# A hybrid SSD and gMLP layer on one core: the scan's TensorE order is paced by blocks of gate logits

## The chip, the cores and the metric

The kernel runs on one core of one Trainium2 chip. A core has TensorE (PE, with its weight loads PEld), VectorE (DVE), ScalarE (ACT), GpSimd (POOL) and SyncE (SP), on whose queue this kernel issues all its DMAs. Each engine works through its own instructions in the order in which they were written, and waits for others by semaphores. The metric is the device time of one execution in microseconds (us).

## The reference

One layer runs over 1152 positions: 1024 latent tokens (8 chunks of 128) and 128 context tokens (a ninth chunk), width 1024. What matters here:

```
P  = h @ w_in                       # z | x,B,C | dt | u,v | gate logits gA,gB
xbc = silu(depthwise_conv(x,B,C))
per chunk, direction, head:  decay = exp(segment sums of dt*a)
  y_diag = (C B^T * decay * dt) x ;  y_off = (C * exp(acum)) h_start
  h_next = exp(a_last) * h + (B * decay_to_end * dt)^T x
y_a = rms_norm((y_fwd + y_bwd + d_skip*x) * silu(z))
u,v = gelu(..) ; v = layer_norm(v) ; y_b = u * (w_spatial v + b)
m  = sigmoid(gA) * (y_a @ w_proj_a) + sigmoid(gB) * (y_b @ w_proj_b)
x  = LN(alpha x + gate1 * (m @ w_out)) ; then a squared-relu MLP and a second LN
```

Latent tokens start from given states, one for each direction; context tokens start from zero, and their final states are outputs.

## The kernel before

Activations lie in SBUF as feature tiles of 128 features by 1152 positions, cut into three blocks of 384 positions. All large products use fp32r operands that are split into a high and a low part, so that one product is three matmuls (`mm3`, L89 to L92). A block of one weight tile is 8 x 3 = 24 matmuls of 128x384 (`fm_block`, L203). Weight tiles of 128x1024 come by DMA (`more_raw`); ScalarE makes the high part and GpSimd or VectorE the low part (`split`, L81 to L87).

The order of the stages: modulation and the first two x/B/C weight tiles, whose products run feature tile by feature tile beside the loading (L373 to L390); the dt chain (`dt_chain`, L415), whose cumulative sums go to DRAM as FB and whose transposes on TensorE (L447) fill QT; ten more x/B/C tiles with convolution and transposes (L465 on); the scan (L528 to L629); the gate logits, 16 weight tiles with 48 blocks of 24 matmuls (L632 to L641), which depend on nothing in the scan; then z (24 blocks), v with its layer norm, u with the spatial product (L743 to L762), the projections and the MLP.

The scan has a backward pass: for chunks 7 to 1 `advance` (L548) multiplies the state `hst` by `eal` on GpSimd (L554), forms the chunk's contribution on TensorE (L551) and adds it on VectorE (L555), while each state is written to DRAM as HB. Then the final states of the context chunk are formed (L562 to L571). The forward pass (L574) goes through chunks 0 to 7 and last the context chunk, each in four steps of four heads, 36 steps in all. One step, on the tiles Fb, Bb (cumulative sums, loaded by DMA and broadcast), Ef and cbD:

```
ACT   Ef = exp(Fb)                    (L599, latent chunks)
DVE   Fb -= QT  (L601);  4x Fb = min(Bb - QT, Fb)  (L604)
POOL  4x cbD = cbU * dt  (L606);  DVE 4x cbD += cbL * dt  (L607)
ACT   Fb = exp(Fb) (L609), Bb = exp(Bb) (L612);  DVE Fb *= cbD (L610)
POOL/DVE Ef *= C (L614, every other step on each), POOL Bb *= C (L615)
PE    y = Fb x + Ef h + Bb h_bwd  (L624);  ACT copies y over x (L626)
```

A scheduler in the framework lays the program out into the engines' queues: it mixes gate-logit matmuls between the scan's small products where it holds the scan's operands to be late. `order(ins, first)` (L140) ties one instruction behind another in that layout without a semaphore. Tiles of a pool rotate over `bufs` buffers; a writer waits until the last reader of its buffer is done.

## Time and profile before

| | |
|---|---|
| runs | 2047.31, 2158.1 and 7596.76 us (median 2158.1) |
| the profiled execution's own time | 2048.03 us |
| its span | 2046.2 us, mean granted TensorE clock 0.982 |
| PE busy | 1932.7 us (94%) |
| DVE busy | 1272.4 us (62%) |
| POOL busy | 689.1 us (34%) |
| ACT busy | 607.1 us (30%) |
| chain that ended last | PE 64%, DVE 22%, DMA 5%, issue 4%, POOL 2%, ACT 2% |

Busy is the time in which an engine had an instruction in work; an engine's successive instructions overlap a little, so that the mean time of one is longer than the step from one start to the next. The chain is followed back from the last instruction to what released it. The shares are means over stages that differ, so the stage that a change touches has to be looked at by itself: the scan lies between about 215 and 541 us of the span, the gate logits between 215 and 557, z from there to about 660, and v and u behind it.

### The profile page before, as it was taken

The page shows a single profiled execution, that of the slowest core. Times are in us where ns is not written, and L with a number is a line of the kernel's source. Part 1 is how long each engine was busy: PE and PEld are TensorE (multiplying, and loading weights), DVE is VectorE, ACT ScalarE, POOL GpSimd, SP SyncE. Part 2 cuts the span into 40 slices and gives each one's busy share as a digit, 9 for nine tenths or more (in the row PEclk, how much of TensorE's full clock was granted, in tenths as well). Part 3 has the DMA queues.
Part 4 walks back from the last instruction along what each step waited for, and adds up shares of the span by engine and source line. Part 5 has one row for each costly group of instructions (what it writes and reads, how often), then busy time and mean ns, then how long its engine had stood idle before and what let it go on. Part 6 is the DMA issues. An engine that isn't in the chain of part 4 may idle for free.

```text
span 2046.2 us, 27658 instructions
## 1 busy us (share of the span) xinstructions
PE 1932.7 (94%) x10669; PEld 1759.5 (86%) x10669; DVE 1272.4 (62%) x2171; ACT 607.1 (30%) x1010; POOL 689.1 (34%) x560
## 2 busy tenths in 40 slices
PE   7999998787899999999999999999999999999886
PEld 4899897676899779999998889899999999988775
DVE  4556837999599534344465875754444444458998
ACT  3333313333322332143232453121221111123423
POOL 0323414767224450046120134511122111135563
PEclk9999999899999999999999999999999999999998
DMA  8145435444485431159544543611111111125432
GB/s 319 34 144 167 169 128 176 117 148 126 131 267 164 135 104 62 42 164 342 160 139 159 199 172 130 223 58 42 42 42 42 48 46 42 42 82 182 138 123 83
DMA packets 110213, 262.47 MB, mean 128 GB/s; under 512 B 11584, under 2 KB 50176, under 8 KB 108928
## 3 DMA queue, kind: packets, MB, share of 16 engines
q1 hardware_dynamic: 110080, 260.70, 38.9%
q8 instruction: 84, 1.38, 0.3%
q14 instruction: 49, 0.40, 0.1%
HBM read 213.30 MB, written 47.35 MB: 127 GB/s over the span
## 4 chain that ended last, share of the span: by engine, by line
PE 64%; DVE 22%; DMA 5%; issue 4%; POOL 2%; ACT 2%; SPq 1%; POOLq 0%; DVEq 0%; ACTq 0%
PE mm_ps L91 20%; PE mm_ps L90 20%; PE mm_ps L92 20%; DVE Fb L604 2%; DVE cbD L607 2%; DMA w_raw<-in_w_ff_dram 1%; DVE crow L282 1%; DVE Fb L601 1%; DMA xg<-NX 1%; DVE w_lo L87 1%; DMA Fb<-FB 1%; DVE Fb L610 1%; DVE xg L934 1%; DVE acc L1021 1%; DVE ln_t L248 1%
## 5 line engine op out<-in xcount | busy, mean ns | idle before, releaser
L87 POOL TENSOR_TENSOR w_lo<-w_raw,w_hi 128x1024 fp32r<-128x1024 f32 x88 | 214.5, 2443 | 517.3 <-ACT w_hi L82 513.7
L82 ACT ACTIVATE w_hi<-w_raw 128x1024 fp32r<-128x1024 f32 (+2 forms) x199 | 205.3, 1039 | 541.5 <-PE mm_ps L92 299.7
L90 PE MATMUL mm_ps<-hTh,w_hi 128*128 128x384 f32 x1056 | 359.4, 344 | 5.7 <-ACT gt L638 3.9
L92 PE MATMUL mm_ps<-hTh,w_lo 128*128 128x384 f32 x1056 | 363.1, 344 | 1.1 <-POOL w_lo L87 1.1
L91 PE MATMUL mm_ps<-hTl,w_hi 128*128 128x384 f32 x1056 | 361.6, 342 | 0.0
L90 PE MATMUL mm_ps<-h,w_hi 128*128 128x384 f32 x768 | 258.9, 338 | 10.5 <-DVE acc L1021 8.9
L92 PE MATMUL mm_ps<-h,w_lo 128*128 128x384 f32 x768 | 258.9, 337 | 5.2 <-POOL w_lo L85 5.2
L91 PE MATMUL mm_ps<-h,w_hi 128*128 128x384 f32 x768 | 258.5, 337 | 0.0
L1021 DVE TENSOR_TENSOR acc<-acc,mm_ps 128x512 f32<-128x512 f32 x240 | 161.1, 684 | 122.9 <-PE mm_ps L92 122.8
L90 PEld LDWEIGHTS mm_ps<-hTh,w_hi 128*128 128x128 f32 x1056 | 200.5, 190 | 15.7 <-issue 6.8
L91 PEld LDWEIGHTS mm_ps<-hTl,w_hi 128*128 128x128 f32 x1056 | 200.7, 190 | 8.4 <-issue 5.9
L92 PEld LDWEIGHTS mm_ps<-hTh,w_lo 128*128 128x128 f32 x1056 | 200.6, 190 | 8.0 <-issue 6.5
L90 PE MATMUL mm_ps<-w_hi,hid 128*128 128x512 f32 x518 | 200.6, 390 | 4.3 <-DVE acc L1021 3.1
L91 PE MATMUL mm_ps<-w_lo,hid 128*128 128x512 f32 x518 | 202.2, 390 | 2.2 <-POOL w_lo L85 2.1
L92 PE MATMUL mm_ps<-w_hi,hid 128*128 128x512 f32 x518 | 201.4, 389 | 0.0
L983 DVE TENSOR_TENSOR rl<-rl 128x384 f32<-128x384 f32 x96 | 112.2, 1170 | 129.3 <-ACT rl L982 129.2
L90 PEld LDWEIGHTS mm_ps<-h,w_hi 128*128 128x128 f32 x768 | 145.6, 190 | 13.3 <-DVE acc L1021 10.1
L92 PEld LDWEIGHTS mm_ps<-h,w_lo 128*128 128x128 f32 x768 | 145.6, 190 | 5.5 <-POOL w_lo L85 5.5
L91 PEld LDWEIGHTS mm_ps<-h,w_hi 128*128 128x128 f32 x768 | 145.6, 190 | 0.7
L87 DVE TENSOR_TENSOR w_lo<-w_raw,w_hi 128x1024 fp32r<-128x1024 f32 (+2 forms) x78 | 94.6, 1216 | 71.9 <-ACT w_hi L82 71.8
L90 PEld LDWEIGHTS mm_ps<-w_hi,hid 128*128 128x128 f32 x518 | 97.4, 188 | 26.4 <-DVE acc L1021 4.4
L91 PEld LDWEIGHTS mm_ps<-w_lo,hid 128*128 128x128 f32 x518 | 97.4, 188 | 24.0 <-POOL w_lo L85 4.1
(260 smaller groups left out, 3550.8 us busy)
## 6 DMA issues: line engine op xcount, KB each, us to landing
w_raw<-in_w_ff_dram SPq DMA_DIRECT2D x93, 512.0 KB, 3.7
w_raw<-in_w_v_dram SPq DMA_DIRECT2D x24, 512.0 KB, 3.6
w_raw<-in_w_out_dram SPq DMA_DIRECT2D x24, 512.0 KB, 3.7
Fb<-FB SPq DMA_DIRECT2D x36, 256.0 KB, 4.0
Bb<-FB SPq DMA_DIRECT2D x36, 256.0 KB, 4.8
GLOG<-gt SPq DMA_DIRECT2D x48, 192.0 KB, 1.9
gin<-GLOG SPq DMA_DIRECT2D x48, 192.0 KB, 3.1
ada_b<-in_w_ada_dram SPq DMA_DIRECT2D x16, 512.0 KB, 7.5
```

The lines of the kernel that those rows point to most:

```text
L82: A.activation(hi, raw, AF.Copy)
L87: eng.tensor_tensor(lo, raw, hi, op=SUB)
L90: T.matmul(ps, s[0], m[0], start=first, stop=False)
L91: T.matmul(ps, s[0], m[1], start=False, stop=False)
L92: T.matmul(ps, s[1], m[0], start=False, stop=last)
L248: V.scalar_tensor_tensor(t, y, x, y, op0=MUL, op1=MUL)
L282: V.scalar_tensor_tensor(wt[:, i, :] if v else junk, wt[:, i, :], 1.0, crow[:, v, :], op0=MUL, op1=MUL, accum_out=outs[:, k, i, v:v + 1])
L601: V.tensor_tensor(Fb, Fb, QT[:, c, 2, h0:h0 + 4].unsqueeze(2).broadcast_to([P, 4, P]), op=SUB)
L604: V.scalar_tensor_tensor(Fb[:, i, :], Bb[:, i, :], QT[:, c, 3, h:h + 1], Fb[:, i, :], op0=SUB, op1=MIN)
L607: V.scalar_tensor_tensor(cbD[:, i, :], cbL[:, g, :], QT[:, c, 0, h:h + 1], cbD[:, i, :], op0=MUL, op1=ADD)
L983: V.tensor_tensor(rl, rl, rl, op=MUL)
L1021: V.tensor_tensor(a, a, ps, op=ADD)
```

## The change

In the scan: (1) the forward pass takes the context chunk first; (2) the state `hst` has two buffers, and `advance` writes the product with `eal` to the new one, on VectorE (it was in place on GpSimd); (3) the four cbD products of a step, the dt weights, are ScalarE copies with a scale (they were GpSimd's); (4) Ef has two buffers for three, cbL and cbU have one for two; (5) the first y product of each step and the first state product of each backward chunk are tied behind a numbered block of gate logits, so that the 36 steps spread over all 48 blocks. Outside it: (6) the spatial product of u is tied behind the last matmul of its own block; (7) the dt transposes are tied behind the fourth x/B/C tile; (8) the third x/B/C weight tile is loaded and split during the start, into a block buffer.

```diff
--- before.py
+++ after.py
@@ -89,7 +89,7 @@
     def mm3(ps, s, m, first, last):
         T.matmul(ps, s[0], m[0], start=first, stop=False)
         T.matmul(ps, s[0], m[1], start=False, stop=False)
-        T.matmul(ps, s[1], m[0], start=False, stop=last)
+        return T.matmul(ps, s[1], m[0], start=False, stop=last)
 
 
     wsrc = []
@@ -115,7 +115,7 @@
     for i in range(len(FIN)):
         fin += [("f1fin", i, (2,))] + [("w2fin", j, None) for j in range(sum(FIN_W2[:i]), sum(FIN_W2[:i + 1]))]
     plan += fin[:2] + [("f2", NCH - NE, (2,))] + fin[2:]
-    homes, HOME = {}, [0, 0, 0, 1, None, None]
+    homes, HOME = {2: 0}, [0, 0, 0, 1, None, None]
     for op, n, bs in plan:
         if op == "f1fin":
             wsrc.append(("ff1", I["w_ff1"][FIN[n]]))
@@ -203,9 +203,11 @@
     def fm_block(pm, w, act, b, evict):
         ps = pm.tile([P, TB], F32, name="mm_ps", tag="mm")
         for k in range(KT):
-            mm3(ps, (w[0][:, k, :], w[1][:, k, :]), (act[b][0][:, k, :], act[b][1][:, k, :]),
-                k == 0, k == KT - 1)
+            done = mm3(ps, (w[0][:, k, :], w[1][:, k, :]), (act[b][0][:, k, :], act[b][1][:, k, :]),
+                       k == 0, k == KT - 1)
+        state["mm"] = done
         evict(b, ps)
+        return done
 
     def fm_tile(pm, w, act, evict, blocks=range(NB)):
         for b in blocks:
@@ -337,7 +339,7 @@
 
 
     lo_eng["eng"] = lambda i: V
-    BEHIND = {KT - 1: (2, 3)}
+    BEHIND = {3: (2,), KT - 1: (3,)}
     fetch_ada(0)
     dma(out=ident, in_=I["ident"])
     dma(out=posr, in_=I["posr"])
@@ -372,6 +374,8 @@
 
     for k in range(KT):
         ht = fetched[k]
+        if k == 5:
+            first.append(take_fm("xbc", 0, 0))
         if k == 2:
             ada_half(1, aux([P, 512], "ada_ps", "tp", 2))
         sc, sh = mod_cols(k, 1)
@@ -411,6 +415,8 @@
     dtv, e1, e2 = (qt[0:R, i * TB:(i + 1) * TB] for i in range(3))
     e3, sf, sb = (qs[0:R, i * TB:(i + 1) * TB] for i in range(3))
     A.activation(dtv, dtp[0:R, :], AF.Identity, bias=dtb[0:R, :])
+
+    late_pe = []
 
     def dt_chain():
         qm = t1_tile("qm")
@@ -444,7 +450,9 @@
         for src, r0, nr, q in ((dtv, 0, 2, 0), (sf, 0, 1, 2), (sb, 1, 1, 3)):
             tp = aux([P, 3, R], "q_ps", "tp", 2)
             for cc in range(3):
-                T.transpose(tp[:, cc, :], src[:, cc * P:(cc + 1) * P], ident[0:R, 0:R])
+                ins = T.transpose(tp[:, cc, :], src[:, cc * P:(cc + 1) * P], ident[0:R, 0:R])
+                if cc == 0:
+                    late_pe.append(ins)
             for cc in range(3):
                 V.tensor_copy(QT.rearrange("p (b c) r h -> p b c r h", c=3)[:, :, cc, q:q + nr, :],
                               tp[:, cc, :].rearrange("p (b r h) -> p b r h", r=2, h=H)[:, :, r0:r0 + nr, :])
@@ -463,7 +471,7 @@
     CT = bcs.tile([P, 2, W], F32, name="CT")
     Bk = bcs.tile([P, NC, 2 * P], F32, name="Bk")
     for n, ft in enumerate((8, 9, 10, 11, 0, 1, 2, 3, 4, 5, 6, 7)):
-        w = take_fm("xbc") if n > 1 else None
+        w = take_fm("xbc") if n > 2 else first[n]
         if ft == 0:
             X = [blk.tile([P, 3, D], F32, name=f"X{b}", tag="blk", bufs=NBLK) for b in range(NB)]
         cv = cvp.tile([P, CW + 2], F32, name="cv", tag="cv", bufs=3)
@@ -485,6 +493,9 @@
                 dt_chain()
         else:
             fm_tile(pmA, w, hT, ev_x)
+            if n == 3:
+                for ins in late_pe:
+                    order(ins, state["mm"])
         t1 = t1_tile("t1")
         w0, w1, w2 = (conv_wc[i][:, ft:ft + 1] for i in range(3))
         G.tensor_scalar(t1, cv[:, 1:1 + CW], w1, conv_bc[:, ft:ft + 1], op0=MUL, op1=ADD)
@@ -535,7 +546,7 @@
         return X[c // 3][:, c % 3, :]
 
     def load_state(src):
-        hs = sp.tile([P, D], F32, name="hst", tag="hst")
+        hs = sp.tile([P, D], F32, name="hst", tag="hst", bufs=2)
         dma(out=hs, in_=src)
         return hs
 
@@ -545,20 +556,28 @@
                         wfb[:, d, c, g * 8:g * 8 + 8].unsqueeze(2).broadcast_to([P, 8, 64]), op=MUL)
         return xw
 
+
+    paced = []
+
     def advance(hs, c, d, xws):
+        new = sp.tile([P, D], F32, name="hst", tag="hst", bufs=2)
         for g in range(2):
             st = aux([P, 512], "st_ps", "st", 1)
-            T.matmul(st, Bk[:, c, g * P:(g + 1) * P], xws[g].rearrange("p h e -> p (h e)"), start=True, stop=True)
-            hg = hs[:, g * 512:(g + 1) * 512]
-            hv = hg.rearrange("p (h e) -> p h e", e=64)
-            G.tensor_tensor(hv, hv, eal[:, d, c, g * 8:g * 8 + 8].unsqueeze(2).broadcast_to([P, 8, 64]), op=MUL)
+            ins = T.matmul(st, Bk[:, c, g * P:(g + 1) * P], xws[g].rearrange("p h e -> p (h e)"), start=True, stop=True)
+            if d == 1 and g == 0:
+                paced.append((ins, NL - 1 - c))
+            hg = new[:, g * 512:(g + 1) * 512]
+            V.tensor_tensor(hg.rearrange("p (h e) -> p h e", e=64),
+                            hs[:, g * 512:(g + 1) * 512].rearrange("p (h e) -> p h e", e=64),
+                            eal[:, d, c, g * 8:g * 8 + 8].unsqueeze(2).broadcast_to([P, 8, 64]), op=MUL)
             V.tensor_tensor(hg, hg, st, op=ADD)
+        return new
 
     hb = load_state(I["h0_b"])
     for c in range(NL - 1, -1, -1):
         dma(out=HB[c], in_=hb)
         if c > 0:
-            advance(hb, c, 1, [xweight(c, 1, g) for g in range(2)])
+            hb = advance(hb, c, 1, [xweight(c, 1, g) for g in range(2)])
     for d in range(2):
         for g in range(2):
             xw = xweight(NL, d, g)
@@ -571,7 +590,8 @@
             dma(out=ov[:, 4 * g:4 * g + 4, :], in_=fs)
 
     hf = load_state(I["h0_f"])
-    for c in range(NC):
+    LEAD = 8
+    for at, c in enumerate([NL] + list(range(NL))):
         lat = c < NL
         if lat:
             hbc = [sp.tile([P, 512], F32, name="hbc", tag="hbc", bufs=2) for _ in range(2)]
@@ -581,8 +601,8 @@
         cbp = aux([P, 2, P], "cb_ps", "tp", 2)
         for g in range(2):
             T.matmul(cbp[:, g, :], BT[:, g, c * P:(c + 1) * P], CT[:, g, c * P:(c + 1) * P], start=True, stop=True)
-        cbL = sp.tile([P, 2, P], F32, name="cbL", tag="cbL", bufs=2)
-        cbU = sp.tile([P, 2, P], F32, name="cbU", tag="cbU", bufs=2)
+        cbL = sp.tile([P, 2, P], F32, name="cbL", tag="cbL", bufs=1)
+        cbU = sp.tile([P, 2, P], F32, name="cbU", tag="cbU", bufs=1)
         V.tensor_tensor(cbL, cbp, mlu[:, 0:1, :].broadcast_to([P, 2, P]), op=MUL)
         V.tensor_tensor(cbU, cbp, mlu[:, 1:2, :].broadcast_to([P, 2, P]), op=MUL)
         for g in range(2):
@@ -595,7 +615,7 @@
                     dma(out=t.rearrange("p h i -> p (h i)"),
                         in_=FB[c, d, h0:h0 + 4, :].rearrange("h i -> (h i)").partition_broadcast(P))
                 if lat:
-                    Ef = sp.tile([P, 4, P], F32, name="Ef", tag="Ef", bufs=3)
+                    Ef = sp.tile([P, 4, P], F32, name="Ef", tag="Ef", bufs=2)
                     A.activation(Ef, Fb, AF.Exp)
                 cbD = sp.tile([P, 4, P], F32, name="cbD", tag="cbD", bufs=2)
                 V.tensor_tensor(Fb, Fb, QT[:, c, 2, h0:h0 + 4].unsqueeze(2).broadcast_to([P, 4, P]), op=SUB)
@@ -603,7 +623,7 @@
                     h = h0 + i
                     V.scalar_tensor_tensor(Fb[:, i, :], Bb[:, i, :], QT[:, c, 3, h:h + 1], Fb[:, i, :],
                                            op0=SUB, op1=MIN)
-                    G.tensor_scalar(cbD[:, i, :], cbU[:, g, :], QT[:, c, 1, h:h + 1], 0.0, op0=MUL, op1=ADD)
+                    A.activation(cbD[:, i, :], cbU[:, g, :], AF.Copy, scale=QT[:, c, 1, h:h + 1])
                     V.scalar_tensor_tensor(cbD[:, i, :], cbL[:, g, :], QT[:, c, 0, h:h + 1], cbD[:, i, :],
                                            op0=MUL, op1=ADD)
                 A.activation(Fb, Fb, AF.Exp)
@@ -621,14 +641,19 @@
                     for n, (lhs, l0, rhs) in enumerate(terms):
                         for i in range(2):
                             j = 2 * qq + i
-                            T.matmul(yp[64 * i:64 * i + 64, q, :], lhs[:, l0 + 64 * j:l0 + 64 * j + 64], rhs[:, j, :],
-                                     start=n == 0, stop=n == len(terms) - 1)
+                            ins = T.matmul(yp[64 * i:64 * i + 64, q, :], lhs[:, l0 + 64 * j:l0 + 64 * j + 64], rhs[:, j, :],
+                                           start=n == 0, stop=n == len(terms) - 1)
+                            if n == i == qq == 0:
+                                e = 4 * at + 2 * g + hh
+                                paced.append((ins, LEAD * (e + 1) // 4 if at == 0 else
+                                              LEAD + (e - 3) * (6 * KT - LEAD) // 32))
                 A.activation(xch(c)[:, (g * 4 + hh * 2) * P:(g * 4 + hh * 2 + 2) * P],
                              yp[:, 2 * hh:2 * hh + 2, :].rearrange("p a b -> p (a b)"), AF.Copy)
         if c < NL - 1:
-            advance(hf, c, 0, xws)
-
-
+            hf = advance(hf, c, 0, xws)
+
+
+    blocks_done = []
     for kind, g0 in (("gb", 8), ("ga", 0)):
         for ft in range(KT):
             w = take_fm(kind)
@@ -638,7 +663,10 @@
                 A.activation(gt, ps, AF.Copy)
                 dma(out=GLOG[g0 + ft][:, b * TB:(b + 1) * TB], in_=gt)
 
-            fm_tile(pmA, w, hT, ev_g)
+            for b in range(NB):
+                blocks_done.append(fm_block(pmA, w, hT, b, ev_g))
+    for ins, n in paced:
+        order(ins, blocks_done[max(0, n - 1)])
     psA.close()
     stA.close()
 
@@ -746,7 +774,9 @@
         def ev_u(b, ps):
             sps = pxB.tile([P, 3, P], F32, name="s_ps", tag="aux")
             for cc in range(3):
-                T.matmul(sps[:, cc, :], Vh[b][:, cc, g * P:(g + 1) * P], WsT[:, g, :], start=True, stop=True)
+                ins = T.matmul(sps[:, cc, :], Vh[b][:, cc, g * P:(g + 1) * P], WsT[:, g, :], start=True, stop=True)
+                if cc == 0:
+                    order(ins, state["mm"])
             ug = tB.tile([P, TB], F32, name="ug", tag="ta", bufs=2)
             A.activation(ug, ps, AF.Gelu)
             sl = tB.tile([P, 3, P], F32, name="sl", tag="tb", bufs=2)
```

What this does to the order, at three places. First TensorE's queue at the end of the scan, where `mm_ps` are gate-logit or z matmuls and `y_ps` the scan's outputs. Before:

```order
L92 MATMUL mm_ps_4837<-hTh2_215,w_lo_4686 128x384
L90 MATMUL mm_ps_4837<-hTh2_215,w_hi_4685 128x384
L624 MATMUL y_ps_3464<-Fb_3490,X2_855 64x128 x4
L91 MATMUL mm_ps_4837<-hTl2_216,w_hi_4685 128x384
L92 MATMUL mm_ps_4837<-hTh2_215,w_lo_4686 128x384
L90 MATMUL mm_ps_4837<-hTh2_215,w_hi_4685 128x384
```

and now:

```order
L91 MATMUL mm_ps_4940<-hTl2_216,w_hi_4788 128x384
L92 MATMUL mm_ps_4940<-hTh2_215,w_lo_4789 128x384
L644 MATMUL y_ps_3451<-Fb_3490,X2_854 64x128 x2
L644 MATMUL y_ps_3451<-Ef_3494,hst_3354 64x128 x2
L644 MATMUL y_ps_3451<-Bb_3491,hbc_3364 64x128 x2
L644 MATMUL y_ps_3451<-Fb_3490,X2_854 64x128 x2
L644 MATMUL y_ps_3451<-Ef_3494,hst_3354 64x128 x2
L644 MATMUL y_ps_3451<-Bb_3491,hbc_3364 64x128 x2
L90 MATMUL mm_ps_5012<-hTh0_211,w_hi_4878 128x384
L91 MATMUL mm_ps_5012<-hTl0_212,w_hi_4878 128x384
```

Before, the last y product had 83 gate-logit matmuls behind it; now the gate logits end before it, and the next row is the first z matmul.

Second ScalarE's queue at the start, from the last high part of the activations (`hTh`): `qt` belongs to the dt chain, `crow` to the modulation, and the `cv` rows empty the accumulators `mm_ps` and `mm2_ps` of the first two weight tiles. Before:

```order
L82 ACTIVATE hTh2_215<-xt_359 128x384
L401 ACT_TABLE_LOAD
L401 ACTIVATE anc_518<-pcol_76 128x1
L413 ACTIVATE qt_523<-dt_ps_223,pcol_76 96x384
L476 ACTIVATE cv_529<-mm_ps_217 128x384
L476 ACTIVATE cv_529<-mm_ps_218 128x384
L476 ACTIVATE cv_620<-mm2_ps_220 128x384
L476 ACTIVATE cv_620<-mm2_ps_221 128x384
```

and now:

```order
L82 ACTIVATE hTh2_215<-xt_359 128x384
L405 ACT_TABLE_LOAD
L405 ACTIVATE anc_523<-pcol_76 128x1
L417 ACTIVATE qt_528<-dt_ps_223,pcol_76 96x384
L430 ACTIVATE qt_528<-qt_528 96x384
L528 ACT_TABLE_LOAD
L528 ACTIVATE crow_960<-crow_960 128x1024
L484 ACTIVATE cv_534<-mm_ps_217 128x384
L484 ACTIVATE cv_625<-mm2_ps_220 128x384
L484 ACTIVATE cv_534<-mm_ps_218 128x384
L484 ACTIVATE cv_625<-mm2_ps_221 128x384
```

The dt chain's exponential, a table load and the `crow` activation moved ahead of the four rows that empty accumulators.

Third TensorE's queue around the first spatial product, `s_ps`; 128x512 matmuls are v, 128x384 are u. Before:

```order
L90 MATMUL mm_ps_6227<-w_hi_6253,hTh1_213 128x512
L90 MATMUL mm_ps_6228<-w_hi_6253,hTh1_213 128x512
L749 MATMUL s_ps_6816<-WsT_6765,V0_5956 128x128 x3
L91 MATMUL mm_ps_6226<-w_lo_6254,hTh1_213 128x512
L92 MATMUL mm_ps_6226<-w_hi_6253,hTl1_214 128x512
L90 MATMUL mm_ps_6226<-w_hi_6253,hTh1_213 128x512
```

and now:

```order
L91 MATMUL mm_ps_6804<-hTl0_212,w_hi_6683 128x384
L92 MATMUL mm_ps_6804<-hTh0_211,w_lo_6684 128x384
L777 MATMUL s_ps_6829<-WsT_6778,V0_5969 128x128 x3
L92 MATMUL mm_ps_6840<-hTh1_213,w_lo_6684 128x384
L90 MATMUL mm_ps_6840<-hTh1_213,w_hi_6683 128x384
```

It stood 39 matmuls behind the end of the first third of v, inside v; now it stands behind the first block of u, 16 blocks' worth of matmuls later.

## Rows read from the trace of the kernel before

**Rows 1.** Busy time of each engine in two stretches (us, instructions), TensorE's granted clock, DMA.

```profile
328.00:541.00 213.00, 174.44 (x1335) 149.12 (x1337) 200.64 (x373) 74.75 (x153) 143.77 (x178) 0.94 0.47 137
541.00:557.00 16.00, 15.05 (x91) 14.56 (x87) 1.23 (x2) 3.90 (x7) 0.00 (x0) 1.00 0.20 70
```

**Rows 2.** The chain of waits (start, us); then line L638, the gate logits' evictions.

```profile
313.82 1.40 PE y_ps L624 x20
...
L638 ACT ACTIVATE gt<-mm_ps x48: 466/477/495, 221.9 to 556.9; 128x384 f32<-128x384 f32 x48
```

**Rows 3.** VectorE's groups from 328 to 541: count, busy us, mean ns, idle before.

```profile
L607 DVE SCALAR_TENSOR_TENSOR cbD<-cbL,QT,cbD 128x128 f32<-128x128 f32 x124 | 62.2, 542 | 2.8 <-POOL cbD L606 2.8
L604 DVE SCALAR_TENSOR_TENSOR Fb<-Bb,QT,Fb 128x128 f32<-128x128 f32 x124 | 56.5, 511 | 0.9 <-DMA Bb<-FB 0.6
L601 DVE TENSOR_TENSOR Fb<-Fb,QT 128x512 f32<-128x512 f32 x31 | 27.3, 879 | 3.6 <-ACT Ef L599 2.5 <-DMA Fb<-FB 0.9
L610 DVE TENSOR_TENSOR Fb<-Fb,cbD 128x512 f32<-128x512 f32 x32 | 24.5, 768 | 0.8 <-ACT Fb L609 0.7
```

**Rows 4.** GpSimd's groups in the same stretch.

```profile
L606 POOL TENSOR_SCALAR cbD<-cbU,QT 128x128 f32<-128x128 f32 x123 | 66.6, 556 | 18.0 <-DVE Fb L610 18.0
L615 POOL TENSOR_TENSOR Bb<-Bb,CT 128x512 f32<-128x512 f32 x28 | 44.9, 1605 | 34.7 <-ACT Bb L612 31.4 <-DVE Fb L604 2.5 <-DVE Ef L614 0.6
L614 POOL TENSOR_TENSOR Ef<-Ef,CT 128x512 f32<-128x512 f32 x13 | 18.9, 1450 | 5.0 <-ACT Ef L599 5.0
L554 POOL TENSOR_TENSOR hst<-hst,eal 128x512 f32<-128x512 f32 x14 | 15.4, 1099 | 0.0
```

**Rows 5.** VectorE's instructions in order of time: start, us.

```profile
415.70 3.99 DVE L607 SCALAR_TENSOR_TENSOR cbD<-cbL,QT,cbD 128x128 f32<-128x128 f32 x4
...
420.21 0.68 DVE L614 TENSOR_TENSOR Ef<-Ef,CT 128x512 f32<-128x512 f32 x1
420.82 1.21 DVE L87 TENSOR_TENSOR w_lo<-w_raw,w_hi 128x1024 fp32r<-128x1024 f32 x1
421.95 1.13 DVE L604 SCALAR_TENSOR_TENSOR Fb<-Bb,QT,Fb 128x128 f32<-128x128 f32 x4
423.00 0.68 DVE L544 TENSOR_TENSOR xw<-X,wfb 128x512 f32<-128x512 f32 x1
```

**Rows 6.** GpSimd's instructions at the first of these.

```profile
415.61 1.32 POOL L614 TENSOR_TENSOR Ef<-Ef,CT 128x512 f32<-128x512 f32 x1
417.11 1.38 POOL L615 TENSOR_TENSOR Bb<-Bb,CT 128x512 f32<-128x512 f32 x1 [0.18 <-DVE cbD L607]
418.45 1.09 POOL L554 TENSOR_TENSOR hst<-hst,eal 128x512 f32<-128x512 f32 x1
```

**Rows 7.** ScalarE: line L378 (ns, least, median, most); then the y evictions from 328 to 541.

```profile
L378 ACT ACTIVATE xt<-xt,mod x8: 478/480/495, 17.3 to 44.9; 128x128 f32<-128x128 f32 x8
...
L626 ACT ACTIVATE X<-y_ps 128x256 f32<-128x256 f32 x35 | 12.9, 370 | 6.9 <-PE y_ps L624 3.5 <-DVE xw L544 3.4
```

**Rows 8.** TensorE's waits from 560 to 830; then its instructions around the first such wait.

```profile
PE s_ps L749 <- DVE V L719: 6.4, 4, 2.5
...
699.13 0.39 PE L91 MATMUL mm_ps<-w_lo,hTh 128*128 128x512 f32 x1
...
708.75 0.80 PE L749 MATMUL s_ps<-WsT,V 128*128 128x128 f32 x2 [2.45 <-DVE V L719]
...
711.05 0.63 PE L92 MATMUL mm_ps<-w_hi,hTl 128*128 128x512 f32 x1
```

**Rows 9.** Start: TensorE's first matmul of the third weight tile, and two of ScalarE's rows.

```profile
66.74 0.45 PE L90 MATMUL mm_ps<-hTh,w_hi 128*128 128x384 f32 x1 [1.85 <-ACT w_hi L82]
...
68.93 1.28 ACT L517 ACT_TABLE_LOAD   x1
70.23 1.06 ACT L517 ACTIVATE crow<-crow 128x1024 f32<-128x1024 f32 x1
```

**Rows 10.** TensorE's waits from 0 to 310.

```profile
PE q_ps L447 <- DVE qs L437: 1.8, 1, 1.8
```

## The prediction

> **What bounds the kernel now.** The page's busy table says TensorE (94%), but it is a mean over stages. I looked for the stretches in which TensorE is not full, with the busy times by window, and then asked the groups of each engine and the waits why. Three places matter.
>
> The first is the forward pass of the scan. The chain reaches its first y product at 313.82 [rows 2]. From 328 to 541 VectorE is busy 200.64 of 213 us, TensorE 174.44 at a mean granted clock of 0.94, ScalarE 74.75, GpSimd 143.77 [rows 1]: VectorE sets the pace. After it, from 541 to 557, TensorE runs alone (15.05 of 16, VectorE 1.23, GpSimd 0): the gate-logit matmuls that were left when the scan ended. The last gate eviction is at 556.9 [rows 2], so z begins at 557. Gate logits could fill TensorE's holes inside the scan, and 16 us of them are spent behind it.
>
> The second is inside VectorE's 200 us. Its mask and dt-weight operations on 128x128 take 542 and 511 ns in the mean [rows 3]. At a moment without GpSimd, four of them take 1.13, and a 128x512 product takes 0.68 with a step of 0.61 to the next [rows 5]. So one step is about 0.263, one latency 0.34, and the rest of the 511 to 542 is stretch. Taking off 0.34 or 0.68 for each: 25 (L607), 21 (L604), 6 (L601) and 3 (L610), together 55 us of 213. Where three GpSimd tensor operations run (1.32 + 1.38 + 1.09), a group of four took 3.99 instead of 1.13 [rows 5, 6].
>
> The third lies outside the scan: TensorE waits 6.4 us for the normalized v in front of spatial products [rows 8], 1.8 at a dt transpose [rows 10], and 1.85 for the third weight tile [rows 9].
>
> **The change part by part. Sum against the profiled execution's 2048.03 us**, which stands 0.7 above the lowest of the runs, 2047.31; their median, 2158.1, is 5% higher because of the spread between them, and I forecast an execution like the profiled one.
>
> *The scan.* Before, 33 of the 36 steps were left at 314 and the last ended near 541: 6.9 us each. Now context comes first, and the four context steps and one latent step go through VectorE during the backward pass, where TensorE has a gate block for each state product and VectorE has room: 31 are left. TensorE has 654 gate matmuls left at that point. The forward pass starts at about 315: 21 more gate matmuls precede it, at 0.17 (15.05 over 91, 16 over 91 [rows 1]) 3.6 us, less about 2 for state products that no longer wait for GpSimd.
>
> VectorE's clean work from there: 31 steps of eight 128x128 at 0.263 and two 128x512 at 0.6 make 102, less 2 for operations already done; 16 Ef products 10; 14 weightings of x, 14 state additions and 12 state multiplications at 0.6, 24; eight low parts of weights at 1.13, 9; seven pairs of masked cb, 5. Sum 148. The state multiplications are the part newly put on VectorE (7 us, and as much in the backward pass, where it is hidden).
>
> On top comes stretch. GpSimd loses the dt weights (66.6) and the state products (15.4) and keeps Bb and its half of Ef, 44.9 + 18.9 [rows 4], for 31 instead of 28 latent steps 70 us. What stretches VectorE isn't settled by the rows. If every GpSimd microsecond counts alike, 55 over 145.8 is 0.38, and 26 us stay. If only GpSimd's tensor-by-tensor operations count, the group of four gives 2.9 over 3.8, 0.75, and about 50 stay. I take the middle, 37, since both kinds were there in nearly every slow group. With 10 idle (12.4 in 213 before), VectorE needs 148 + 37 + 10 = 195, bounds 184 and 207. The scan ends at 510, its last y takes 1.4 [rows 2], and no gate logits are left behind it: z begins at 512 instead of 557. **Minus 45**, from -56 to -33.
>
> Is TensorE able to follow? 654 x 0.17 = 111, 32 y groups at 1.4, 45, states and cb 8: 165 of the 195. Yes, with 30 spare.
>
> ScalarE gets 144 copies. An eviction of 128x256 without pointers takes 370; 128x128 with two pointers takes 478 to 495 [rows 7]. One pointer on 128 columns lies between, 0.26 (370 less the 107 that the gate eviction's 128 columns more cost, 477 [rows 2]) and 0.48; at 0.36 that is 1.4 us per step on an engine that is busy 75 of 213. Not the bound, but its queue is in order: behind a copy that waits for cbU or for a cbD buffer stand the two exponentials of that step, the next exp(Fb), and the gate evictions. The copies' wait is the same that GpSimd had; who waits for it now is new (a rival below).
>
> By the Trainium skill, "ScalarE: Activation LUTs", section "What ACT_TABLE_LOAD costs", a copy of 128 columns with one pointer would take some 0.39, about 0.29 back to back, an estimate of 42 us for the 144 copies; the two-pointer figure it gives agrees with the 478 to 495 here. The same page's "Rules for kernel authors" would have multiplications on VectorE and not on ScalarE, which speaks against this part; here VectorE is the engine without room.
>
> Ef with two buffers for three, cbL and cbU with one for two: at no cost as long as ScalarE's exp(Fb) is a step ahead; if that cover goes, see the rivals.
>
> *Spatial products.* Two waits, together 6.4 us in four entries at two places, the longest 2.45 at 708.75; behind it 128x512 matmuls take 0.63 instead of 0.39 [rows 8] for about 13 matmuls, 3 us. Tied behind the first block of u, 277 matmuls later, V is long ready. 6.4 + 2 x 3 = 12; I allow 8 to 13, as the second wait is shorter. **Minus 12.** Nothing is late next: the product of the gate in u needs it only with its own block's eviction.
>
> *dt transposes*: the 1.8 goes [rows 10]. **Minus 2.** QT comes later, but is needed only in the scan.
>
> *Third weight tile early.* The 1.85 wait for its high part goes [rows 9]. But ScalarE's four rows that empty the accumulators now stand behind the dt exponential, a table load (1.28) and crow (1.06) [rows 9], and TensorE, with three accumulators, waits for one of these instead: 1.28 + 1.06 + about 0.5 less 1.85, **plus 1**, -3 to +3. The reordered loads on SyncE's queue and the extra low part on VectorE lie beside TensorE's products.
>
> Sum: -45 - 12 - 2 + 1 = -58, **1990 us**; own range 1976 to 2006.
>
> **The rivals.**
> *TensorE becomes the bound (0.13).* All stretch goes with the dt weights, if those alone made it: VectorE needs 148 + 10, and TensorE's 165 decides. z begins at 315 + 165 + 2 = 482, and the sum is -75 - 13 = 1960 to 1965. For: L607 sits right behind L606, and GpSimd was busy with L606 longest. Against: the slow group stood beside L614, L615 and L554, not L606 [rows 5, 6]. The Trainium skill, "SBUF — State Buffer", section "SBUF: two separate sides", says that VectorE with two SBUF inputs and a reading GpSimd block each other wholly, one for the whole length of the other; by this all 82 us taken off GpSimd would come back, up to TensorE's bound. The trace shows less: 55 lost beside 145.8.
>
> *The step keeps its 6.9 us (0.17).* The scan is then bound by the round over ScalarE: Fb's exponential, four copies, two more exponentials and a y copy, in one queue, with fewer Ef buffers. 31 x 6.9 = 214: z at 530, -27 - 13 = 2008. For: 2.5 of L601's 3.6 idle us already wait for ScalarE's Ef [rows 3]. Against: ScalarE is busy 35%.
>
> *Slower (0.04).* The tied y products put a serial chain in TensorE's order: y frees Ef, the exponential two steps on may start, then ScalarE's copies, exp of Fb and Bb, GpSimd's Bb product at 1.6 [rows 4], the next y. Behind the waiting y stand 21 gate matmuls that can't pass it, 3.6 us; so they add to the chain instead of filling it. If the chain is 1.4 for y, 3.6 for the matmuls, 1.4 for the copies, two exponentials at about 0.7 (a 128x512 by the 0.107 per 128 columns from the 0.37 of 128x256 is 0.58) and 1.6 for Bb, it is 9.4 us a step: the scan takes 291, z begins at 606, and the time is 2048 + 49 - 13 = 2084. It decides from a step of (557 + 13 - 315) / 31 = 8.2 us on. Against: the y products are tied to block counts, and the operands of two steps lie ahead.
>
> *The ties do little (0.04)*: the layout was as good before, only the waits outside go; 2035.
>
> **How the numbers follow.** Forecast 0.62 (1976 to 2006), TensorE bound 0.13 (1960 to 1965), step kept 0.17 (2000 to 2020), slower 0.04, little 0.04. The range 1967 to 2022 holds the forecast and the kept step, and leaves out most of the TensorE case and the last two, about 0.2. Two per cent, about what a measurement of this kernel can tell from no change, is 41 us: faster means under 2007. That is the forecast, the TensorE case and a little under half of the kept step, less the forecast's upper edge: 0.79. Slower needs 2089, the far end of its case: 0.03. The rest, 0.18, is within 2%.
>
> **What would show it.** Right: z's first matmul near 512; no stretch with VectorE idle and TensorE on gate logits behind the last y; L604 and L607 near 0.4 in the mean, GpSimd about 70 us in the forward pass; TensorE's clock there nearer to 1; no wait at s_ps and q_ps. Wrong: L604 and L607 still above 0.5 with GpSimd halved (the tensor products make the stretch); y waiting long for Bb or Ef with ScalarE or GpSimd as the releaser (the round); z near 482 (TensorE). The third tile is right if TensorE's longest wait between 60 and 75 names a ScalarE row that empties an accumulator.

## The result, and the profile after

The changed kernel takes 1995.72 us (median of four executions, 1993.56 to 1998.1), 0.9747 of the kernel before, with an interval of 0.9723 to 0.977: 52 us less on 2048. Two executions of before were disturbed and raise its plain median; the ratio leaves them out, as do all ratios below. The forecast was 1990, 58 us less. The total is near by luck: two terms were wrong in opposite directions, and what I named as the cause of the larger one is only a part of it.

The profiled execution has a span of 1996.3 us, 49.9 less than before. First the busy times from the beginning of the gate logits to z (columns as in [rows 1]; the order is TensorE, its weight loads, VectorE, ScalarE, GpSimd, then TensorE's granted clock; the second window ends a microsecond into z):

```profile
215.00:311.30 96.30, 95.44 (x546) 87.63 (x546) 59.19 (x117) 32.52 (x70) 7.55 (x2) 1.00 0.51 173
311.30:517.70 206.40, 185.83 (x1454) 160.36 (x1449) 190.18 (x381) 116.36 (x278) 74.66 (x46) 0.98 0.50 142
```

Then the line of the gate logits' evictions, as in [rows 2]:

```profile
L663 ACT ACTIVATE gt<-mm_ps x48: 466/473/494, 213.1 to 516.2; 128x384 f32<-128x384 f32 x48
```

And VectorE's groups inside the forward pass, 320 to 511, with GpSimd's behind them (count, busy us, mean ns, idle before; compare [rows 3, 4]):

```profile
L624 DVE SCALAR_TENSOR_TENSOR Fb<-Bb,QT,Fb 128x128 f32<-128x128 f32 x119 | 54.3, 510 | 1.1 <-DMA Bb<-FB 0.9
L627 DVE SCALAR_TENSOR_TENSOR cbD<-cbL,QT,cbD 128x128 f32<-128x128 f32 x112 | 42.9, 429 | 3.3 <-ACT cbD L626 3.3
L621 DVE TENSOR_TENSOR Fb<-Fb,QT 128x512 f32<-128x512 f32 x29 | 22.5, 775 | 2.9 <-ACT Ef L619 2.8
L573 DVE TENSOR_TENSOR hst<-hst,st_ps 128x512 f32<-128x512 f32 x14 | 9.5, 676 | 0.0
L570 DVE TENSOR_TENSOR hst<-hst,eal 128x512 f32<-128x512 f32 x12 | 8.9, 770 | 0.0
```

```profile
L635 POOL TENSOR_TENSOR Bb<-Bb,CT 128x512 f32<-128x512 f32 x29 | 48.1, 1659 | 73.4 <-ACT Bb L632 52.3 <-DVE Fb L624 9.9 <-DVE hst L573 6.5
L634 POOL TENSOR_TENSOR Ef<-Ef,CT 128x512 f32<-128x512 f32 x14 | 22.9, 1633 | 47.5 <-ACT Ef L619 47.5
```

What the reader sees: the gate logits begin at 213.1 instead of 221.9, 8.8 us earlier; the forward pass begins at 311.3 instead of 313.8, so 6.3 of the 8.8 are used up before it; z's first matmul starts at 516.8 instead of 557.4. From the first gate eviction to that matmul it was 335.5 us and is 303.7: 31.8 less. From there to the end, 9.3 less: 8.8 + 31.8 + 9.3 = 49.9. VectorE still sets the pace (190 of 206), and the mask operations (L624) are as slow with half of GpSimd's work gone as they were before, 510 ns against 511.

### The profile page after: what moved, and what is told of

Same layout as the page of the kernel before. It is cut to its first block, busy times and chain, and to the rows that moved or that the text cites. A ratio compares the mean times of both kernels' runs of the same rounds, so it can differ in the third digit from the quotient of the medians.

```text
span 1996.3 us, 27629 instructions
## 1 busy us (share of the span) xinstructions
PE 1917.7 (96%) x10669; PEld 1749.4 (88%) x10669; DVE 1263.2 (63%) x2200; ACT 651.7 (33%) x1154; POOL 590.0 (30%) x387
## 4 chain that ended last, share of the span: by engine, by line
PE 67%; DVE 18%; DMA 7%; issue 4%; ACT 2%; POOL 2%; SPq 1%; POOLq 0%; ACTq 0%; DVEq 0%
PE mm_ps L90 21%; PE mm_ps L91 21%; PE mm_ps L92 21%; DMA w_raw<-in_w_ff_dram 2%; DVE Fb L624 2%; ACT w_hi L82 1%; DVE rl L1013 1%; DVE cbD L627 1%; DMA xg<-NX 1%; PE y_ps L644 1%; DVE w_lo L87 1%; DVE crow L284 1%; DMA ada_w<-in_w_ada_dram 1%; DVE xg L964 1%; DVE w_lo L85 1%
## 5 line engine op out<-in xcount | busy, mean ns | idle before, releaser
L90 PE MATMUL mm_ps<-hTh,w_hi 128*128 128x384 f32 x1032 | 355.3, 348 | 0.9 <-ACT gt L663 0.9
L92 PE MATMUL mm_ps<-hTh,w_lo 128*128 128x384 f32 x1032 | 350.6, 340 | 0.7 <-DVE w_lo L87 0.7
L91 PE MATMUL mm_ps<-hTl,w_hi 128*128 128x384 f32 x1032 | 350.3, 339 | 0.0
L90 PEld LDWEIGHTS mm_ps<-hTh,w_hi 128*128 128x128 f32 x1032 | 195.4, 190 | 11.1 <-issue 7.9
L91 PEld LDWEIGHTS mm_ps<-hTl,w_hi 128*128 128x128 f32 x1032 | 194.7, 189 | 9.5 <-issue 7.0
L92 PEld LDWEIGHTS mm_ps<-hTh,w_lo 128*128 128x128 f32 x1032 | 194.5, 188 | 5.3 <-issue 4.3
```

The lines of the kernel that those rows point to most:

```text
L90: T.matmul(ps, s[0], m[0], start=first, stop=False)
L91: T.matmul(ps, s[0], m[1], start=False, stop=False)
L92: return T.matmul(ps, s[1], m[0], start=False, stop=last)
```

## The experiments

Seventeen kernels ran. The effect of each is given in us as the difference of two ratios to before, times 2048; the interval of one ratio is 6 to 11 us wide from end to end, so a difference of less than some 5 to 7 us can't be told from none.

| kernel | ratio to before | interval | against the changed kernel |
|---|---|---|---|
| the change | 0.9747 | 0.9723 to 0.977 | |
| dt weights back on GpSimd (cbd_pool) | 0.983 | 0.9808 to 0.9852 | +17 |
| one state buffer, in place (hst_inplace) | 0.9808 | 0.979 to 0.9826 | +12 |
| spatial products as before (spat_off) | 0.9795 | 0.9768 to 0.9822 | +10 |
| third weight tile as before (third_back) | 0.979 | 0.9773 to 0.9808 | +9 |
| third tile and dt transposes as before (outer_off) | 0.9784 | 0.977 to 0.9799 | +8 |
| context last, ties kept (ctx_last) | 0.9774 | 0.9752 to 0.9796 | +6 |
| context last, no ties (ctx_pace_off) | 0.9766 | 0.9752 to 0.9781 | +4 |
| state product on GpSimd (hst_pool) | 0.9758 | 0.9732 to 0.9784 | +2 |
| dt transposes as before (dt_off) | 0.9754 | 0.9739 to 0.9768 | +1 |
| no ties (pace_off) | 0.9751 | 0.9733 to 0.977 | +1 |
| all products on VectorE (all_dve) | 0.9679 | 0.9657 to 0.97 | -14 |
| and a subtraction on ScalarE (dve_sub_act) | 0.9629 | 0.9608 to 0.9649 | -24 |
| the same without ties (best_nopace) | 0.9633 | 0.9613 to 0.9654 | -23 |

| before, plus | ratio | interval | against before |
|---|---|---|---|
| dt weights on ScalarE (b_cbd) | 0.9984 | 0.9968 to 1.0 | -3 |
| second state buffer (b_hst) | 0.9958 | 0.9943 to 0.9972 | -9 |
| both (b_cbd_hst) | 0.9938 | 0.9914 to 0.9962 | -13 |
| both, state product on VectorE (b_scan) | 0.9872 | 0.9845 to 0.9898 | -26 |

**What stretches VectorE.** First the dt weights taken back:

```
-                    A.activation(cbD[:, i, :], cbU[:, g, :], AF.Copy, scale=QT[:, c, 1, h:h + 1])
+                    G.tensor_scalar(cbD[:, i, :], cbU[:, g, :], QT[:, c, 1, h:h + 1], 0.0, op0=MUL, op1=ADD)
```

> The changed kernel with the dt weights cbD back on GpSimd, all else as changed. Theory (VectorE paces the forward pass, and a GpSimd product stretches it only while a scalar_tensor_tensor wants to start): the 124 dt weights give back about 20 us of stretch to VectorE, less 3 us of waits for ScalarE: 2008 to 2016 us. Rival (the gain of the scan comes from taking the dt weights off GpSimd): 2026 or more. Rival (the ties alone did it): 1996.

17 us more, inside the theory's range, but not all by the theory's term. From the forward pass to z (311.6 to 530.8) the profiled execution is 14 us longer: VectorE is busy 200.5 us instead of 189.3, 11 more and not 20, and sits idle some 2.5 more. Then the other side, GpSimd taken out of the scan:

```
-                    (V if hh else G).tensor_tensor(Ef, Ef, ctb, op=MUL)
-                    G.tensor_tensor(Bb, Bb, ctb, op=MUL)
+                    V.tensor_tensor(Ef, Ef, ctb, op=MUL)
+                    V.tensor_tensor(Bb, Bb, ctb, op=MUL)
```

> The changed kernel with all Ef and Bb products of the scan on VectorE, none on GpSimd. Theory (a GpSimd product blocks VectorE's scalar_tensor_tensor for 0.86 us each): VectorE gets 43 products at 0.61, 26 us, and loses 37 us of stretch: scan 11 us shorter, 1985 us, the 128x128 operations at 0.34 ns-thousands mean instead of 0.51 and 0.43. Rival (work moved onto the bound engine counts in full, the stretch has another cause): 2015 to 2022.

1980.75 us, 14 less, although the bound engine got 43 more products (the expectation's "0.34 ns-thousands" is 0.34 us). VectorE's groups of that kernel, from 320 to 500:

```profile
L627 DVE SCALAR_TENSOR_TENSOR cbD<-cbL,QT,cbD 128x128 f32<-128x128 f32 x113 | 33.3, 342 | 0.9 <-ACT cbD L626 0.9
L624 DVE SCALAR_TENSOR_TENSOR Fb<-Bb,QT,Fb 128x128 f32<-128x128 f32 x116 | 33.3, 342 | 1.5 <-DMA Bb<-FB 1.5
L621 DVE TENSOR_TENSOR Fb<-Fb,QT 128x512 f32<-128x512 f32 x29 | 19.9, 685 | 5.9 <-ACT Ef L619 5.6
L573 DVE TENSOR_TENSOR hst<-hst,st_ps 128x512 f32<-128x512 f32 x14 | 9.5, 678 | 0.0
L570 DVE TENSOR_TENSOR hst<-hst,eal 128x512 f32<-128x512 f32 x12 | 7.7, 684 | 1.0 <-PE y_ps L644 1.0
```

342 ns where it was 510 and 429: the 0.34 that the prediction took from one clean group is the duration without GpSimd. How the block looks is seen in the changed kernel, VectorE's instructions from 399 and GpSimd's beside them (start, us):

```profile
399.98 1.65 DVE L624 SCALAR_TENSOR_TENSOR Fb<-Bb,QT,Fb 128x128 f32<-128x128 f32 x2
401.56 0.86 DVE L627 SCALAR_TENSOR_TENSOR cbD<-cbL,QT,cbD 128x128 f32<-128x128 f32 x3
402.34 0.68 DVE L573 TENSOR_TENSOR hst<-hst,st_ps 128x512 f32<-128x512 f32 x1
402.94 0.68 DVE L555 TENSOR_TENSOR xw<-X,wfb 128x512 f32<-128x512 f32 x1
403.54 1.35 DVE L627 SCALAR_TENSOR_TENSOR cbD<-cbL,QT,cbD 128x128 f32<-128x128 f32 x1
```

```profile
399.48 1.75 POOL L635 TENSOR_TENSOR Bb<-Bb,CT 128x512 f32<-128x512 f32 x1 [2.20 <-DVE Fb L624]
402.89 1.84 POOL L635 TENSOR_TENSOR Bb<-Bb,CT 128x512 f32<-128x512 f32 x1 [1.67 <-ACT Bb L632]
```

The single L627 that starts at 403.54 ends at 404.89, where GpSimd's product ends (404.73); alone it takes 0.34. The two L624 last until 401.63, GpSimd's product until 401.23. An operation that reads two SBUF tiles and starts behind such a product waits it out: of the mask and dt-weight operations that start between 320 and 511, 32 start inside a product's record, and they take 0.78 to 1.39; all others take 0.34 to 0.35. The wait goes the other way too: the weighting of x (L555, 402.94) takes its clean 0.68 inside the record of a product that is 1.84 long, where the shortest takes 1.26. The addition to the state (L573), which reads one operand from PSUM, takes 676 and 678 in both kernels. The Trainium skill, "SBUF — State Buffer", section "SBUF: two separate sides", says just this: two SBUF inputs against a reading GpSimd, and whoever is second waits wholly. These rows agree.

The dt weights cost much less. I call stretch the time beyond what an operation takes without GpSimd. Counting (mean - 342), (mean - 682) or, for the low parts of weights, (mean - 1216) times the count over the groups from 320 to 511, VectorE's stretch is 38 us beside 71 us of GpSimd in the changed kernel, 0.54 per us. With the dt weights back it is 45 beside 118, in the kernel before 56 beside 137. At 0.54 for the 62 and 77 us of tensor products, 11 and 14 us are left for 56 and 60 us of dt weights: 0.2 per us. Counted by the GpSimd records that each stretched operation overlaps, it is 10 and 11 us; in cbd_pool an operation that meets only dt weights, mostly of 0.40 us, mostly takes 0.45. Of the prediction's two readings, the one by tensor products was the better; that the middle of both, 37, came out at 38 is luck, since the tensor products cost 0.54 per us and not 0.75.

**What the scan's gain consists of.** The ties and the place of the context chunk:

```
-    for ins, n in paced:
-        order(ins, blocks_done[max(0, n - 1)])
```

> The changed kernel without the ties of y and state products to gate blocks. Theory: gate logits are again used up unevenly and a tail of TensorE work alone comes back behind the scan, up to 16 us: 2004 to 2012 us. Rival (the layout does as well by itself, now that context comes first): 1996. Rival (the ties hold products back that are ready): below 1990.

No effect: the layout spreads the y products as well without them. The second rival holds.

```
-    for at, c in enumerate([NL] + list(range(NL))):
+    for at, c in enumerate(range(NC)):
```

> The changed kernel with the context chunk last again in the forward pass, ties kept (the first chunk's steps tied to the first 8 blocks). Theory (VectorE's work from the forward pass on sets the end; context first lets four steps of about 3.3 us run while TensorE paces the backward pass): 13 to 18 us more, 2008 to 2014 us, and VectorE less busy before the forward pass. Rival (the ties keep the tail away, whatever comes last): 1996.

Below the theory's range: 6 us, and the two intervals overlap. The latent steps begin at 288.7 in that kernel and the context's end at 520.8: what is saved ahead is paid behind. With both edits:

> The changed kernel with the context chunk last and without the ties. Theory (context first and the ties both keep gate logits from being left over, either one is enough): the tail of gate logits behind the scan is back, 10 to 16 us above the kernel with context last and ties (2003): 2013 to 2019 us. Rival (the tail came from the dt weights on GpSimd alone): 2003, no tail.

4 us, no tail of gate logits: my theory fell here, and the rival's explanation, the dt weights, fell with the next run, which makes the prediction's main argument alone on the kernel before (the edit is the reverse of cbd_pool's).

> The kernel before with the dt weights on ScalarE and nothing else changed. Theory (VectorE paces the scan there too, and loses about 20 us of stretch; the tail of gate logits stays): 2028 to 2035 us. Rival (without context first and the ties the scan gets shorter and the tail as much longer): 2042 to 2047.

3 us, hardly to be told from none, instead of the 12 to 19 expected; the last y ends 4 us earlier in its trace, and the tail of 16 us behind it stays. VectorE's stretch from 320 to 511 is 51 us there, against 56 before; 88 us of GpSimd's tensor products, the state's among them, are enough to keep it (the product of Fb with cbD is at 1027 ns on average):

```profile
L607 DVE SCALAR_TENSOR_TENSOR cbD<-cbL,QT,cbD 128x128 f32<-128x128 f32 x108 | 49.8, 511 | 0.0
L604 DVE SCALAR_TENSOR_TENSOR Fb<-Bb,QT,Fb 128x128 f32<-128x128 f32 x116 | 49.7, 485 | 0.7 <-DMA Bb<-FB 0.7
L610 DVE TENSOR_TENSOR Fb<-Fb,cbD 128x512 f32<-128x512 f32 x29 | 29.7, 1027 | 0.1
```

```profile
L554 POOL TENSOR_TENSOR hst<-hst,eal 128x512 f32<-128x512 f32 x14 | 17.7, 1264 | 4.2 <-PE y_ps L624 4.2
```

What I had not read in the trace of before are GpSimd's waits ahead of the forward pass (total us, times, longest), 215 to 314:

```profile
POOL hst L554 <- DMA HB<-hst: 37.5, 5, 8.0
POOL cbD L606 <- DVE cbU L587: 14.4, 1, 14.4
```

The state is written to DRAM (HB) while the next product is to overwrite it in place; the product waits for that DMA. With a second buffer VectorE waits 0.3 us for HB in the changed kernel. One buffer put back into the changed kernel:

```
-        hs = sp.tile([P, D], F32, name="hst", tag="hst", bufs=2)
+        hs = sp.tile([P, D], F32, name="hst", tag="hst")
...
-        new = sp.tile([P, D], F32, name="hst", tag="hst", bufs=2)
+        new = hs
```

> The changed kernel with one state buffer, the product with eal in place again (on VectorE as in the change). Theory (the second buffer is what the scan gained most by: the product no longer waits for the DMA that writes the old state to HB, 37.5 us of waits in the backward pass before): the forward pass begins later and VectorE stands in line behind that wait, 15 to 25 us more: 2011 to 2021 us. Rival (the backward pass is TensorE's anyway, gate blocks fill it): 1996 to 2000.

12 us, a little under the range; VectorE waits 9.8 us for HB there, the forward pass begins at 318.6. The same on the kernel before, where the three buffers given up pay for it:

```
+        new = sp.tile([P, D], F32, name="hst", tag="hst", bufs=2)
...
-            hg = hs[:, g * 512:(g + 1) * 512]
...
+            hg = new[:, g * 512:(g + 1) * 512]
...
-        cbL = sp.tile([P, 2, P], F32, name="cbL", tag="cbL", bufs=2)
-        cbU = sp.tile([P, 2, P], F32, name="cbU", tag="cbU", bufs=2)
+        cbL = sp.tile([P, 2, P], F32, name="cbL", tag="cbL", bufs=1)
+        cbU = sp.tile([P, 2, P], F32, name="cbU", tag="cbU", bufs=1)
...
-                    Ef = sp.tile([P, 4, P], F32, name="Ef", tag="Ef", bufs=3)
+                    Ef = sp.tile([P, 4, P], F32, name="Ef", tag="Ef", bufs=2)
```

> The kernel before with two state buffers (product still on GpSimd, to the new buffer) and with Ef, cbL and cbU a buffer fewer, which pays for it. Theory: the backward pass loses its waits for HB, the forward pass begins up to 18 us earlier, and as VectorE paces it the end moves by most of that: 2030 to 2036 us. Rival (alone it does nothing, as the dt weights alone did nothing: both are needed): 2042 to 2048.

9 us: between the two, the first latent y comes at 292.8 instead of 313.8, but the end gains less than half of that. GpSimd still waits 16.2 us for HB there, in two entries. What the three buffers cost by themselves no run shows. Both parts together:

> The kernel before with both: two state buffers and the dt weights on ScalarE. By the kernel with context last and no ties (2000), less the spatial products (13) and the start (7), and with the product on GpSimd instead of VectorE (3): 2020 to 2024 us. Rival (the gain of the scan hangs on the gate logits' beginning earlier): 2035 or more.

13 us, the rival's number. The parts so far simply add up (3 + 9), and about 15 us of the scan's 32 were still unaccounted for (32 less 13, and less the 4 of the context chunk and the ties). The one part left was the engine of the state's product, which on the changed kernel had hardly mattered:

```
-            V.tensor_tensor(hg.rearrange("p (h e) -> p h e", e=64),
+            G.tensor_tensor(hg.rearrange("p (h e) -> p h e", e=64),
```

> The changed kernel with the state's product with eal on GpSimd again, into the new buffer. Theory (14 products of 0.6 leave VectorE in the forward pass, but each GpSimd product blocks it for about as long): 1993 to 1999 us, no difference. Rival (the product on VectorE was a gain in itself): 2003 or more. Rival (it only cost VectorE): 1988.

No difference that can be told. But added to the kernel before, with the other two:

> The kernel before with the dt weights on ScalarE, two state buffers and the state's product on VectorE: the scan of the change without context first and without ties, nothing outside the scan. Theory (the product on GpSimd is what kept both from adding up: it blocks VectorE like Ef and Bb): by the kernel with context last and no ties (2000) and the spatial products (13) and start (7) on top, 2018 to 2024 us, VectorE's stretch near 39 us. Rival (the scan's gain needs the gate logits to begin earlier): 2033 or more, as with the product on GpSimd.

26 us, as the theory said, and VectorE's stretch at 36 us (47 without it). The first rows of VectorE from 320 to 511:

```profile
L606 DVE SCALAR_TENSOR_TENSOR Fb<-Bb,QT,Fb 128x128 f32<-128x128 f32 x116 | 51.8, 499 | 1.4 <-DMA Bb<-FB 1.2
L609 DVE SCALAR_TENSOR_TENSOR cbD<-cbL,QT,cbD 128x128 f32<-128x128 f32 x112 | 42.0, 421 | 3.8 <-ACT cbD L608 3.8
```

So three edits of the scan make 26 of its 32 us: the dt weights off GpSimd, the state's product off GpSimd, and its second buffer. Why the last step is worth 13 on the kernel before and 2 on the changed one isn't settled. Each of the two differences has some 7 us of uncertainty, so a part can be noise; the stretch in hst_pool is 46 us, 8 more than in the changed kernel, for 8 us of products taken off VectorE, and in b_cbd_hst it is 11 more than in b_scan, hardly another amount.

**Outside the scan.** The spatial products without their tie:

```
-                if cc == 0:
-                    order(ins, state["mm"])
```

> The changed kernel without the tie of the spatial products: the two waits for the normalized v come back, 6.4 us and the slow matmuls behind them. By the forecast's term 12 us: 2008. By the trace after, in which z to the end is 10.6 us shorter: 2006. Rival (only the waits count, the slow clock doesn't): 2002.

10 us, near the 9.3 that z to the end lost (the expectation's 10.6 counts from a microsecond into z), and the wait of [rows 8] is back word for word in its size:

```profile
PE s_ps L777 <- DVE V L747: 6.4, 4, 2.5
```

The start, first both edits and then each:

```
-    homes, HOME = {2: 0}, [0, 0, 0, 1, None, None]
+    homes, HOME = {}, [0, 0, 0, 1, None, None]
...
-    BEHIND = {3: (2,), KT - 1: (3,)}
+    BEHIND = {KT - 1: (2, 3)}
...
-        if k == 5:
-            first.append(take_fm("xbc", 0, 0))
...
-        w = take_fm("xbc") if n > 2 else first[n]
+        w = take_fm("xbc") if n > 1 else None
...
-            if n == 3:
-                for ins in late_pe:
-                    order(ins, state["mm"])
```

> The changed kernel with the third weight tile and the dt transposes as before. Theory (TensorE bounds the time from the first gate block to the forward pass, so the 8.8 us that the gate logits begin earlier go on in full): 2003 to 2005 us. Rival (the forward pass takes its start from the chain of states, whatever TensorE gained before): 1997 to 1999. As forecast, 1 us: 1997.

> The changed kernel with the third x/B/C weight tile loaded and split as before, the dt transposes still late. Theory (most of the 8.8 us at the start is the third tile: with it gone TensorE again waits 1.85 us at 65 and runs thinly to 80, at a granted clock under 1): gate logits begin 5 to 7 us later, 2001 to 2003 us. As forecast (the tile costs 1 us): 1995.

> The changed kernel without the tie of the dt transposes, the third tile still early. Theory (the wait of 1.8 us at the transpose comes back, with some slow matmuls behind it): 1998 to 1999 us. Rival (with the third tile's matmuls in front the layout keeps the transposes late by itself): 1996, no wait at q_ps.

8, 9 and 1 us: it is the third tile, whose time is a little above its expected 2001 to 2003. Without their tie the dt transposes wait 0.3 and 0.2 us, not 1.8, as the rival has it: with the third tile's matmuls in front the layout keeps them late by itself. TensorE in the window from 64 to 80, before, then the changed kernel, then the changed kernel without the third tile early (columns as above):

```profile
64.00:80.00 16.00, 13.04 (x65) 12.39 (x64) 12.35 (x15) 8.24 (x16) 8.55 (x14) 0.89 0.23 67
```

```profile
64.00:80.00 16.00, 16.00 (x94) 16.00 (x93) 15.93 (x12) 5.33 (x13) 11.25 (x10) 1.00 0.21 66
```

```profile
64.00:80.00 16.00, 13.02 (x58) 12.37 (x57) 11.71 (x14) 7.88 (x15) 8.34 (x13) 0.79 0.23 67
```

94 matmul rows instead of 65 and 58: the wait of 1.85 was the larger part of 3 us in which TensorE idled (a wait of 1.1 for the tile's low part from GpSimd is the rest), and the granted clock of these 16 us was 0.89 (0.79), a mix of the two levels.

**A faster version.** With GpSimd out, VectorE had 179 of the 192 us from the forward pass to z. One more operation goes to ScalarE (`nq2` holds the negative of the subtracted column):

```
-                V.tensor_tensor(Fb, Fb, QT[:, c, 2, h0:h0 + 4].unsqueeze(2).broadcast_to([P, 4, P]), op=SUB)
...
+                    A.activation(Fb[:, i, :], Fb[:, i, :], AF.Identity, bias=nq2[:, c, h:h + 1])
```

> The kernel with all Ef and Bb products on VectorE, and the first subtraction of a step (128x512 on VectorE) as four ScalarE activations of 128x128 with a bias. Theory (VectorE still paces the scan at 192 us and TensorE needs some 177): VectorE loses 31 x 0.61 = 19 us, the scan becomes TensorE's at about 490 instead of 503: 1965 to 1970 us. Rival (the round over ScalarE's queue, eight short operations more on it in two steps, sets the step now): 1981 or more.

1972.74 us, 0.9629 of before. The time is 3 to 8 us above the expectation, the mechanism holds: from the forward pass to z TensorE has no wait and no slow clock,

```profile
312.00:490.00 178.00, 178.00 (x1419) 155.76 (x1416) 158.49 (x390) 147.53 (x394) 0.00 (x0) 1.00 0.57 165
```

and VectorE has 20 us to spare. Without the ties:

> The fastest kernel so far (all products on VectorE, the first subtraction on ScalarE) without the ties to gate blocks. Theory (TensorE waits for nothing from 312 to 490 there; the ties do nothing): 1971 to 1975 us. Rival (with VectorE near its end too, the layout alone leaves a tail or a hole): 1980 or more.

0.9633, the same: with TensorE as the bound they do nothing either.

## Why the prediction was right and wrong, step by step

**The step that failed is the scan's term, "minus 45", and its cause.** From the first gate eviction to z the change brought 31.8, outside the term's own -56 to -33. Of the 13 us missing, 5 lie ahead of the forward pass and 8 in it. The pieces:
- VectorE's stretch was taken as 37 and is 38 to 39: right in size, though the split between its two readings was a guess. Its clean work was taken as 148; 189.3 busy less the stretch leaves 151, and with all products on VectorE it is busy 179.3 with 43 more products at 0.61 (26), which leaves 153. Its idle time was taken as 10 and is 16 (3.3 for ScalarE's cbD, 2.8 for Ef, 4.6 for high parts of weights, 2.8 and 0.9 for DMAs, 1.2 for an exponential). From its first latent y to z the forward pass takes 205.5 instead of 195 + 2.
- The start of the forward pass was taken as 3.6 - 2 later in gate-logit work; it is 6.3. TensorE is full there (95.4 of 96.3), and the context's y products, which I had left out, stand in it.
- "The state products that no longer wait for GpSimd", priced at 2: they waited 37.5 us for the DMA to HB. The second buffer is worth 9 to 12. The prediction had no row on it, since I read GpSimd's busy time [rows 4] and not its waits ahead of 314.
- The dt weights were the argument's center. Alone they bring 3, with the other parts in 17 (cbd_pool), and their share of the stretch is 0.2 per us of GpSimd.
- Context first and the ties were to make the tail of [rows 1] vanish. It vanishes without both (ctx_pace_off, 4 us), once the scan's other parts are in.

**The start, "plus 1" for the third tile**, is -9, and this is a second failed step. I had ScalarE's exponential, table load and crow ahead of the rows that empty the accumulators, and took their time as in [rows 9]. But what ScalarE waited for comes earlier: the last dt product ran at 63.1 before and at 54.3 now, and so ScalarE was through with all three before the rows were due:

```profile
57.02 1.28 ACT L528 ACT_TABLE_LOAD   x1
58.32 1.06 ACT L528 ACTIVATE crow<-crow 128x1024 f32<-128x1024 f32 x1
60.84 1.99 ACT L484 ACTIVATE cv<-mm_ps 128x384 f32<-128x384 f32 x4 [1.47 <-PE mm_ps L92]
```

The row was read right and its place in time was not. And I counted the wait of 1.85 alone, without the 1.1 for the low part and without the slow clock, though I had counted that for the spatial products.

**Right:** spatial products, -12 forecast, -10 measured (range 8 to 13). dt transposes: the 1.8 us are gone, though not through their tie. ScalarE's copies: 390 ns each (0.26 to 0.48 was the range, 0.36 taken); they make VectorE wait 3.3 us. The 390 agrees with the estimate of 0.39 from the Trainium skill, "ScalarE: Activation LUTs", section "What ACT_TABLE_LOAD costs". The rule to multiply on VectorE, from its section "Rules for kernel authors", is not tested here, since no run has the dt weights there; moving a subtraction from VectorE to ScalarE (dve_sub_act) made the kernel 10 us faster.

**The rivals.** TensorE as the bound of the scan did not come with this change, though with VectorE's 190 us cut to 158 (dve_sub_act) it does. The kept step of 6.9 us: it is 205.5 / 31 = 6.6, halfway to the forecast's 6.3; but the cause is not that rival's round over ScalarE, as VectorE is busy 189 of the 205.5 us and waits about 7 for ScalarE's Ef, cbD and exponential. The ties that do little: true of the ties, though not of the rest. The slower case did not occur; in the whole forward pass TensorE waits 4.0 us for Fb and 1.3 for Bb, and 11.6 ahead of y products for nothing that the profile names.

## What to carry to other kernels

Read the waits of every engine ahead of a stage, not only its busy time: a product in place that waits for the DMA of the old value is seen only there. Beside a busy VectorE, a GpSimd tensor product can cost VectorE more than doing it itself; compare an operation's mean with its duration in a group without GpSimd before dividing work between the two. When a wait is removed, count the slow clock around it as well, and when a step moves, move also the things it was waiting for.

## What was unexpected of the hardware

- A GpSimd product of 128x512 from SBUF costs VectorE 0.54 us per us on average (38 beside 71), a GpSimd multiplication of 128x128 by a scalar about 0.2. VectorE's additions with an operand in PSUM stayed at 674 to 682 ns throughout.
- In 16 us with 3 us of idle TensorE's granted clock was 0.89 in one kernel and 0.79 in another, with 29 and 36 fewer matmul rows than in 16 us without idle at the full clock.
